# Eight softmax products of layer 0 go from VectorE to GpSimd, and the routing splits h earlier

## The chip, the cores and the metric

The kernel runs on one core of a Trainium2 chip. The metric is the device time of one execution in microseconds, as the median of several runs. Engines are named as the profile names them: PE (TensorE; PEld is its weight load), DVE (VectorE), ACT (ScalarE), POOL (GpSimd) and SP (SyncE, which issues most of the DMAs). L442 is line 442 of the kernel before.

## The reference

Two decoder layers over one sequence of 256 tokens with a model width of 1024. Layer 0's attention joins three branches: attention over compressed blocks, over selected blocks and over a window, each with a gate. Layer 1's attention is one masked softmax over all blocks. Behind each attention stands a mixture of 32 experts in 4 groups, of which a token takes one group and two experts, and then a gate with a per-layer embedding. Cut to what the change touches:

```python
# layer 0: two of the branches, a softmax each, scaled by a gate
p = exp(s - max(s)); p = p / sum(p)
o = gate_c * o_c + gate_s * (p_s @ v) + gate_w * (p_w @ v)
# routing, both layers
x = rms_norm(h, g_ffn)
scores = x @ w_router + bias           # 32 experts and 4 groups
group  = argmax(group scores); two best experts of that group
out   += sum over the two: weight * expert(x)
```

## The kernel before

**The whole.** Tokens lie in two query tiles of 128 rows (t = 0, 1). The program is written once, in order, with a tile framework: a scheduler decides when the program is built in which order each engine runs its instructions, and a pool of buffers decides which tile lies where. `tc.issue_after(x)` tells the scheduler to place what follows behind x. On the chip each engine runs its own list in that fixed order, and waits for semaphores where a tile isn't ready.

**Layer 0's attention** (`attend`, with nbr=2 branches) goes over eight chunks c of two heads (b = 0, 1). `scores` (L409 to L412, PE) multiplies queries by keys for chunk c+1; `turn` transposes the probabilities of chunk c on PE (L455 for p0, the first query tile; L456 and L457 for the two halves of p1, the second query tile) and copies them, L460 on ACT and L461 on DVE; `values` (L473 and L487, PE) multiplies them by the values. Between them stands `softmax`: for each head DVE adds the mask and takes the extreme (L429), ACT takes the exponential and its sum (L431), DVE makes the coefficients (L434 reciprocal, L436 times the gates), and each probability tile is multiplied by its coefficient. A head has four such products: p0 is 128x128 and p1 128x256, with two branches br each. In layer 0 the products of p0 run on POOL (L442) and those of p1 on DVE (L440). In layer 1 (nbr=1) all run on DVE.

In the same stage other work fills the engines: L301, L309, L311 and L315 normalise later queries, L340 splits weights into two parts (tiles wsp), L351 to L353 are products with split operands, L537 with L540 is the output projection, L571 a piece of the embedding's projection, L763 and L722 belong to the compressed branch.

**Routing** (both layers; L826 and on). h lies as rows of tokens. `transposed(t)` takes the mean square of h (ACT, L259 to L263: Square, Ln, Exp), transposes h on PE (L891) and copies the halves, L895 on DVE and L893 on ACT. `logits` multiplies by the router (L905) and DVE scales (L907). `choose(t)` finds group and experts on DVE (L913 to L923, the tile A marks the two experts). `order(t)` counts on PE (L936, L938) and makes each token's rank in its expert (L939), and `place` writes a 0/1 matrix from it (L929, tile rs). `gather_first` (L970, PE) gathers the tokens of the first eight experts with it; its other operand is h in two parts: h_hi, a cast of h (`split_h`, L948, ACT), and h_lo, what the cast leaves (`rest_h`, L951, DVE). Later L1021 gathers the others. L1045 (ACT) and L1047 (DVE) scale what was gathered, L1059 to L1088 make the experts' weights, L1094 and L1095 count tokens per expert, and `second_helping` finds experts with more than 32 tokens; the number of them, noveri (L1160), decides by a branch (L1308) if a leftover pass is run. Then `gate_up` (L1185) and `down` (L1215 to L1234) run over eight groups j of four experts, whose weights SP's queue loads (L840 gate and up, 1 MB each; L100 down, 0.5 MB).

The lines that set the two places are these:

```python
if t or nbr == 1:                    # softmax: which engine multiplies
    nc.vector.tensor_scalar(...)
else:
    mark["pool", c] = nc.gpsimd.tensor_scalar(...)
...
with tc.issue_after(nc.vector.tensor_tensor(A[:, t], A2[:, t, 0], A2[:, t, 1], ALU.add).ins):
    rest_h(t)                        # end of choose(t)
```

Of the kernel before, what the change touches and what calls it, by code (L numbers as in the profile page):

```python
# [15 lines left out]
ALU = mybir.AluOpType  # L16
# [23 lines left out]
def hybrid_kernel(ctx: ExitStack, tc: tile.TileContext, I: dict, out: bass.AP, dbg=None):  # L40
    nc = tc.nc
# [15 lines left out]
    def pa(shape, dt=F32):  # L57
        return ps.tile(shape, dt, tag="pa", name=nm("pa"))

    def pb(shape, dt=F32):  # L60
        return ps.tile(shape, dt, tag="pb", name=nm("pb"))

    def bt(tag, shape, dt=F32):

        return big.tile(shape, dt, tag=tag, name=nm(tag))

    def wt(tag, shape, dt=F32, bufs=None):
        return wk.tile(shape, dt, tag=tag, name=nm(tag), bufs=bufs)

    def st(tag, shape, dt=F32, bufs=None):  # L70
        return sm.tile(shape, dt, tag=tag, name=nm(tag), bufs=bufs)
# [183 lines left out]
    def columns(t):  # L255

        return hh[0][:, t, :].rearrange("q (k p) -> q k p", k=NK)

    def inv_rms(t, ss, rstd):  # L259
        junk = wt("sq", [P, D], BF16)  # L260
        nc.scalar.activation(junk, hh[0][:, t, :], AF.Square, accum_out=ss[:, t:t + 1])
        nc.scalar.activation(rstd[:, t:t + 1], ss[:, t:t + 1], AF.Ln, scale=1.0 / D, bias=eps_c)
        last_act.append(nc.scalar.activation(rstd[:, t:t + 1], rstd[:, t:t + 1], AF.Exp, scale=-0.5))  # L263
# [152 lines left out]
    def softmax(c, nbr, raw, gates=None):  # L416

        a, i = divmod(c, 4)
        ws = []
        for b in range(2):  # L420
            hh = 8 * a + 4 * b + i
            s0, s1 = raw[b]
            p1 = wt("p1", [P, nbr, S], bufs=4)
            p0 = wt("p0", [P, nbr, P], bufs=4)
            mx = st("mx", [P, NT, nbr], bufs=4)
            sums = st("sums", [P, NT, nbr], bufs=4)
            for t, (pt_, st_, dt_) in enumerate(((p0, s0, d_q0), (p1, s1, d_q1))):
                for br in range(nbr):
                    nc.vector.tensor_tensor_reduce(pt_[:, br, :], st_[:, br, :], dt_, -SLOPE[hh], 3e38,  # L429
                                                   ALU.add, ALU.min, accum_out=mx[:, t, br:br + 1])  # L430
                    mark["exp", c] = nc.scalar.activation(pt_[:, br, :], pt_[:, br, :], AF.Exp, bias=mx[:, t, br:br + 1],  # L431
                                         scale=-1.0, accum_out=sums[:, t, br:br + 1])
            cf = st("cf", [P, NT, nbr], bufs=4)
            nc.vector.reciprocal(cf, sums)  # L434
            if gates is not None:
                nc.vector.tensor_tensor(cf, cf, gates[:, :, 3 * hh + 1:3 * hh + 3], ALU.mult)  # L436
            for t, pt_ in enumerate((p0, p1)):
                for br in range(nbr):
                    if t or nbr == 1:
                        nc.vector.tensor_scalar(pt_[:, br, :], pt_[:, br, :], cf[:, t, br:br + 1], None, ALU.mult)  # L440
                    else:
                        mark["pool", c] = nc.gpsimd.tensor_scalar(pt_[:, br, :], pt_[:, br, :], cf[:, t, br:br + 1],  # L442
                                                                  None, ALU.mult)
            ws.append((p0, p1))
        return ws
# [54 lines left out]
    def attend(fill, after, nbr, qs, k1, k2, V, oT, gates=None, cmp=None):  # L500

        mark.clear()
        ws = softmax(0, nbr, scores(0, nbr, qs, k1, k2), gates)
        for c in range(8):
            fill(c)
            if nbr == 1:
                pts = turn(nbr, ws)
            if c < 7:
                raw = scores(c + 1, nbr, qs, k1, k2)
            if nbr == 2:  # L510
                pts = turn(nbr, ws)
            if c < 7:
                ws = softmax(c + 1, nbr, raw, gates)
            values(c, nbr, pts, V, oT, cmp)
            after(c)
# [86 lines left out]
    for j in range(2):  # L602
        pt = X.scaled(pts[j], "p1", 4)
# [74 lines left out]
    for c in range(2):  # L678
        pt = pb([P, P])
# [146 lines left out]
    def moe(l, out_proj_tail, prefetch):  # L826
# [38 lines left out]
        hT = bt("X3", [P, NK, S])  # L865
# [11 lines left out]
        A2 = st("A2", [P, NT, 2, NE], BF16, bufs=1)  # L877
        A = st("A", [P, NT, NE], BF16, bufs=1)
# [5 lines left out]

        def transposed(t):
            ts_ = slice(t * P, (t + 1) * P)
            inv_rms(t, ss, rstd)
            for k0 in range(0, NK, 4):
                pt = pa([P, 4, P])
                for k in range(4):  # L890
                    i = nc.tensor.transpose(pt[:, k, :], columns(t)[:, k0 + k, :], ident)  # L891
                if k0:
                    c = nc.scalar.copy(hT[:, k0:k0 + 4, ts_], pt)  # L893
                else:
                    nc.vector.tensor_copy(hT[:, k0:k0 + 4, ts_], pt)  # L895
            return i, c

        pls = {}
# [1 line left out]
        def logits(t, half):  # L900
            ts_ = slice(t * P, (t + 1) * P)
            if half == 0:
                pls[t] = pa([P, NE + NG])
            for k in range(4 * half, 4 * half + 4):
                i = nc.tensor.matmul(pls[t], hT[:, k, ts_], wr[:, l, k, :], start=(k == 0), stop=(k == NK - 1))  # L905
            if half == 1:
                nc.vector.scalar_tensor_tensor(lg[:, t, 0:NE + NG], pls[t], rstd[:, t:t + 1], rb[:, l, :], ALU.mult,  # L907
                                               ALU.add)
            return i

        def choose(t):

            nc.vector.max(gm[:, t], lg[:, t, NE:NE + 8])  # L913
            nc.vector.max_index(gi[:, t], gm[:, t], lg[:, t, NE:NE + 8])
            nc.vector.tensor_tensor(pen[:, t], iota_e[:, 0:NG], gi[:, t, 0:1].to_broadcast([P, NG]), ALU.not_equal)
            nc.vector.scalar_tensor_tensor(le[:, t].rearrange("p (g e) -> p g e", g=NG),
                                           pen[:, t, :, None].to_broadcast([P, NG, 8]), -BIG,
                                           lg[:, t, 0:NE].rearrange("p (g e) -> p g e", g=NG), ALU.mult, ALU.add)
            nc.vector.max(em[:, t], le[:, t])
            nc.vector.max_index(ei[:, t], em[:, t], le[:, t])  # L920
            nc.vector.tensor_tensor(A2[:, t], iota_e[:, None, :].to_broadcast([P, 2, NE]),
                                    ei[:, t, 0:2, None].to_broadcast([P, 2, NE]), ALU.is_equal)
            with tc.issue_after(nc.vector.tensor_tensor(A[:, t], A2[:, t, 0], A2[:, t, 1], ALU.add).ins):  # L923
                rest_h(t)

        def place(i, t):
            if t == 0:
# [19 lines left out]
        def split_h(t):  # L947
            nc.scalar.copy(h_hi[:, t], columns(t))  # L948

        def rest_h(t):  # L950
            nc.vector.tensor_tensor(h_lo[:, t], columns(t), h_hi[:, t].bitcast(F32), ALU.subtract)  # L951
# [22 lines left out]
        for n in range(2):  # L974
            out_proj_tail(0, n)
        out_proj_tail(1, 0)
        _, c = transposed(0)
        add, i = out_proj_tail(1, 1)
        with tc.issue_after(i.ins):
            i = logits(0, 0)  # L980
        with tc.issue_after(c.ins):
            split_h(0)
        with tc.issue_after(i.ins):
            i, c = transposed(1)
        with tc.issue_after(i.ins):
            i = logits(0, 1)
        with tc.issue_after(add.ins):
            choose(0)
        with tc.issue_after(c.ins):
            split_h(1)  # L990
        with tc.issue_after(i.ins):
            for k in range(2):
                i = logits(1, k)
# [8 lines left out]
        with tc.issue_after(i.ins):  # L1002
            for k0 in (0, 2):
                i = gather_first(0, k0)
        dump(f"h{1 + 3 * l}", hh[0])
        choose(1)
        with tc.issue_after(i.ins):
            i = order(1)
# [342 lines left out]
    def ple(B, X, nxt=None):  # L1351
# [36 lines left out]
        if nxt:  # L1388
            act_tables(EXP_LN, last_act[-1])

    B_p, X = moe(0, tail_a, lambda: load_ple(0))
    gm1 = g_mix[:, 1, :]
    B_kv = Weights(I["w_kv"], g_kv)
# [58 lines left out]

    attend(fill_b, after_b, 1, qs, k1, k2, V, oT)
    B_p, X = moe(1, partial(wo[0].add, 3), lambda: load_ple(1))
    dump("h5", hh[0])
    ple(B_p, X)
# [71 lines left out]
```

## Time and profile before

| what | value |
|---|---|
| median of 3 runs | 527.64 us (526.7 to 532.3) |
| profiled execution | 526.64 us, of which the span of the instructions is 524.9 |
| PE busy | 501.8 us (96%) |
| DVE busy | 339.8 us (65%) |
| ACT busy | 278.3 us (53%) |
| POOL busy | 50.9 us (10%) |
| granted clock of PE | 0.999 over the span |

The profile is of one execution. Busy is the time in which an engine had an instruction in work; waits are idle time of an engine just before an instruction, put down to what came last. Starts in the timeline are in us from the span's start. An entry such as "x2" in the timeline joins two neighbouring instructions of one form, and its time goes from the first's start to the last's end.

### The profile page before, as it was taken

How to read it: one execution, taken by the hardware profiler on the slowest of the kernel's cores; microseconds unless marked ns; L12 is line 12 of the kernel's file. 1: busy time of each engine (PE TensorE's matmuls, PEld its weight loads, DVE VectorE, ACT ScalarE, POOL GpSimd, SP SyncE). 2: the span in 40 equal slices, each digit the busy share in tenths (PEclk: the TensorE clock that was granted, in tenths of full speed). 3: DMA queues.
4: the chain of work that ended last, by engine and by line, in shares of the span. 5: the costliest groups of instructions: out<-in, count | busy, mean ns of one | idle time of the engine just before them, and what ended most of it. 6: DMA issues, size and time to landing. Idle time of an engine off the chain costs nothing. (4 is left out here: it accounts for less than half of the span.)

```text
span 524.9 us, 10142 instructions
## 1 busy us (share of the span) xinstructions
PE 501.8 (96%) x3784; PEld 355.7 (68%) x3784; DVE 339.8 (65%) x1038; ACT 278.3 (53%) x650; POOL 50.9 (10%) x120
## 2 busy tenths in 40 slices
PE   9989999999899999999899999999999999998996
PEld 6969899567568665555458999856567656554486
DVE  6759968989974853424269975787749525241593
ACT  6839747985654342312369975664444412231691
POOL 5000402234330001100000000000000003000000
PEclk9999999999999999999999999999999999999999
DMA  8976650006778899999993789632459899999902
GB/s 338 420 294 261 219 227 2 1 1 235 292 293 313 319 421 417 408 418 418 389 405 126 228 312 361 244 158 81 182 198 339 343 418 421 417 415 409 386 4 80
DMA packets 32213, 147.16 MB, mean 280 GB/s; under 512 B 4001, under 2 KB 4273, under 8 KB 22305
## 3 DMA queue, kind: packets, MB, share of 16 engines
q1 hardware_dynamic: 31232, 144.39, 70.6%
q0 software_dynamic: 784, 2.05, 1.0%
q8 instruction: 31, 0.51, 0.4%
q14 instruction: 22, 0.17, 0.1%
q10 hardware_dynamic: 144, 0.04, 0.0%
HBM read 146.98 MB, written 1.05 MB: 282 GB/s over the span
## 5 line engine op out<-in xcount | busy, mean ns | idle before, releaser
L131 DVE SCALAR_TENSOR_TENSOR wsp<-raw,vec,wsp 128x512 fp32r<-128x512 f32 (+1 forms) x96 | 67.1, 747 | 3.3 <-ACT wsp L130 3.2
L130 ACT ACTIVATE wsp<-raw,vec 128x512 fp32r<-128x512 f32 (+1 forms) x96 | 62.9, 719 | 2.3 <-DMA raw<-in_w_c_dram 1.6
L1185 PE MATMUL pb<-wgu,X 128*32 128x256 f32 x768 | 52.0, 381 | 0.6 <-PEq L1308 0.6
L431 ACT ACTIVATE p<-p,mx 128x128 f32<-128x128 f32 (+1 forms) x96 | 42.6, 445 | 10.2 <-DVE mx L429 10.1
L819 ACT ACTIVATE p<-pb,srs 128x128 f32<-128x128 f32 x16 | 5.9, 368 | 71.1 <-PE pb L1185 64.1
L1185 PEld LDWEIGHTS pb<-wgu,X 128*32 128x32 f32 x768 | 27.3, 110 | 18.5 <-issue 2.9
L340 DVE TENSOR_TENSOR pta<-pb,p 128x512 fp32r<-128x512 f32 (+1 forms) x36 | 24.7, 688 | 22.6 <-ACT p L340 18.1
L353 PE MATMUL pa<-XA,wsp 128*128 128x256 f32 x128 | 36.3, 284 | 2.1 <-DVE wsp L131 2.1
L351 PE MATMUL pa<-XA,wsp 128*128 128x256 f32 x128 | 37.2, 291 | 0.7 <-DVE rs L301 0.7
L822 DVE TENSOR_TENSOR p<-pb,ptb 128x128 f32<-128x128 f32 (+1 forms) x18 | 5.2, 289 | 48.4 <-ACT ptb L821 46.2
L352 PE MATMUL pa<-XB,wsp 128*128 128x256 f32 x128 | 36.2, 283 | 0.0
L340 ACT CAST p<-pb 128x512 fp32r<-128x512 f32 (+1 forms) x36 | 21.0, 586 | 27.8 <-PE pb L1234 27.8
L442 POOL TENSOR_SCALAR p<-p,cf 128x128 f32<-128x128 f32 x32 | 25.7, 815 | 65.6 <-DVE cf L436 46.8
L460 ACT COPY pta<-pa 128x512 f32<-128x512 f32 (+1 forms) x32 | 14.8, 479 | 30.4 <-PE pa L456 30.3
L429 DVE CUSTOM_DVE_ANT_0 p<-pb,d_q 128x128 f32<-128x128 f32 (+1 forms) x96 | 29.3, 351 | 2.2 <-PE pb L410 1.0
L1234 PE MATMUL pb<-wd,hT 128*32 128x512 f32 x224 | 29.3, 597 | 1.2 <-issue 0.4
L537 PE MATMUL pa<-wo,XH 128*128 128x512 f32 x64 | 29.4, 602 | 0.0
L1021 PE MATMUL pb<-rs,X 128*128 128x256 f32 (+1 forms) x192 | 26.6, 292 | 0.0
L1021 PEld LDWEIGHTS pb<-rs,X 128*128 128x128 f32 x192 | 24.3, 188 | 2.6 <-issue 2.5
L353 PEld LDWEIGHTS pa<-XA,wsp 128*128 128x128 f32 x128 | 24.1, 189 | 2.5 <-DVE wsp L131 2.5
L351 PEld LDWEIGHTS pa<-XA,wsp 128*128 128x128 f32 x128 | 24.1, 189 | 1.9 <-DVE rs L301 0.9
L352 PEld LDWEIGHTS pa<-XB,wsp 128*128 128x128 f32 x128 | 24.1, 189 | 0.5 <-issue 0.5
(373 smaller groups left out, 1348.6 us busy)
## 6 DMA issues: line engine op xcount, KB each, us to landing
wgu<-in_moe_gu_dram SPq DMA_DIRECT2D x48, 1024.0 KB, 11.8
wd<-in_moe_w_down_dram SPq DMA_DIRECT2D x48, 512.0 KB, 9.6
wo<-in_w_out_dram SPq DMA_DIRECT2D x8, 1024.0 KB, 4.7
raw<-in_ple_gate_dram SPq DMA_DIRECT2D x16, 512.0 KB, 7.0
raw<-in_a_q_dram SPq DMA_DIRECT2D x8, 512.0 KB, 7.3
XB<-in_moe_gu_dram SPq DMA_DIRECT2D x4, 1024.0 KB, 5.7
XA<-in_moe_gu_dram SPq DMA_DIRECT2D x4, 1024.0 KB, 6.8
X<-in_moe_gu_dram SPq DMA_DIRECT2D x4, 1024.0 KB, 5.3
```

The lines of the kernel that those rows point to most:

```text
L130: nc.scalar.activation(hi, src, AF.Copy, scale=g)
L131: nc.vector.scalar_tensor_tensor(lo, src, g, hi.bitcast(F32), ALU.mult, ALU.subtract)
L340: return nc.scalar.copy(hi, src), eng.tensor_tensor(lo, src, hi.bitcast(F32), ALU.subtract)
L351: nc.tensor.matmul(o, a[0], b[0], start=first, stop=False)
L352: nc.tensor.matmul(o, a[0], b[1], start=False, stop=False)
L353: return nc.tensor.matmul(o, a[1], b[0], start=False, stop=last)
L429: nc.vector.tensor_tensor_reduce(pt_[:, br, :], st_[:, br, :], dt_, -SLOPE[hh], 3e38, ALU.add, ALU.min, accum_out=mx[:, t, br:br + 1])
L431: mark["exp", c] = nc.scalar.activation(pt_[:, br, :], pt_[:, br, :], AF.Exp, bias=mx[:, t, br:br + 1], scale=-1.0, accum_out=sums[:, t, b ...
L537: m = nc.tensor.matmul(pt, self.oT[0][:, 2 * j + i, t * P:(t + 1) * P], self.raw[j][:, i, n * 512:(n + 1) * 512], start=(i == 0), stop=(i ...
L1021: nc.tensor.matmul(pt, part_columns(x, t)[:, k, :], Gs[i][:, t, 0:e1], start=(t == x == 0), stop=(t == x == 1))
L1185: last_ = nc.tensor.matmul(gu[32 * i:32 * i + 32, 0:2], xg[:, k, 32 * i:32 * i + 32], wgu[i][k], start=(k == 0), stop=(k == NK - 1), tile_ ...
L1234: behind[:] = [nc.tensor.matmul(ysp[32 * i:32 * i + 32, :], hT[:, 32 * i:32 * i + 32], wd[i][n], start=True, stop=True, tile_position=(0, ...
```

## The change

The condition in `softmax` leaves layer 1 as it is; in layer 0 DVE keeps, of the products of p1, only those with b=0 or br=0. The product for b=1, br=1 goes to POOL: one 128x256 product in each of the eight chunks. In the routing of both layers, `split_h(t)` is called first in `transposed(t)` instead of behind the copies, and `rest_h(t)` is placed behind DVE's copy in `transposed(t)` instead of behind the end of `choose(t)`.

```diff
                 for br in range(nbr):
-                    if t or nbr == 1:
+                    if (t and not b * br) or nbr == 1:
                         nc.vector.tensor_scalar(pt_[:, br, :], pt_[:, br, :], cf[:, t, br:br + 1], None, ALU.mult)
                     else:
...
         def transposed(t):
             ts_ = slice(t * P, (t + 1) * P)
+            split_h(t)
             inv_rms(t, ss, rstd)
...
-                    nc.vector.tensor_copy(hT[:, k0:k0 + 4, ts_], pt)
+                    d = nc.vector.tensor_copy(hT[:, k0:k0 + 4, ts_], pt)
+            with tc.issue_after(d.ins):
+                rest_h(t)
             return i, c
...
-            with tc.issue_after(nc.vector.tensor_tensor(A[:, t], A2[:, t, 0], A2[:, t, 1], ALU.add).ins):
-                rest_h(t)
+            nc.vector.tensor_tensor(A[:, t], A2[:, t, 0], A2[:, t, 1], ALU.add)
...
-        with tc.issue_after(c.ins):
-            split_h(0)
...
-        with tc.issue_after(c.ins):
-            split_h(1)
```

The scheduler's order changes with it, at three places that the prediction speaks of. The first is PE's order in layer 0's attention, at chunk c=1: p_164 and p_163 are p0 and p1 of head b=0, p_169 and p_168 those of b=1, and L311 with L409 and L410 begins the work for chunk c=2.

```order
+L487 MATMUL pa_1235<-X_46_396 128x256
 L455 MATMUL pa_1280<-ident,p_164_1198 128x128
-L763 MATMUL pb_1244<-ident,sq_1145 128x128 x2
+L456 MATMUL pa_1280<-ident,p_163_1197 128x128
+L455 MATMUL pa_1280<-ident,p_164_1198 128x128
+L456 MATMUL pa_1280<-ident,p_163_1197 128x128
+L457 MATMUL pa_1281<-ident,p_163_1197 128x128 x2
+L455 MATMUL pa_1292<-ident,p_169_1217 128x128
+L456 MATMUL pa_1292<-ident,p_168_1216 128x128
+L455 MATMUL pa_1292<-ident,p_169_1217 128x128
+L456 MATMUL pa_1292<-ident,p_168_1216 128x128
 L311 MATMUL pb_1255<-sq_1253,blk_114 128x512
```

The transposes of both heads, up to the last L456 of p_168, moved ahead of L311; before, all but the first stood behind the scores L409 to L412 of c=2.

The second place is DVE's order in layer 1's routing around the rank of the second token tile. Before (A is the choice of the second tile, X_994 is h_lo, es and ep belong to the experts' weights, rs is the matrix of `place`):

```order
-L921 TENSOR_TENSOR A_990_4702<-iota_e,ei_4700 128x64
-L923 TENSOR_TENSOR A_4703<-A_990_4702 128x32
-L951 TENSOR_TENSOR X_994_4706<-XA_2999,X_993_4705 128x1024
-L939 SCALAR_TENSOR_TENSOR rank_4704<-pa_4819,A_4703 128x32
-L1068 TENSOR_REDUCE es_4899<-ep_4893 128x2
-L929 TENSOR_TENSOR rs_4795<-rank_4704,iota_s 128x256
```

After, in the changed kernel's line numbers (L941 is the rank, L931 `place`):

```order
+L1069 TENSOR_REDUCE es_4899<-ep_4893 128x2
+L1070 TENSOR_TENSOR es_4899<-es_4899,gs_4897 128x2
+L1071 RECIPROCAL es_4899<-es_4899 128x2
+L1073 TENSOR_TENSOR cb_4906<-ep_4893,es_4899 128x4
+L1076 TENSOR_TENSOR oh_4701<-A_990_4702,cb_4906 128x2x32 x2
+L1078 TENSOR_TENSOR cw_4908<-oh_4701 128x64
+L1085 CAST R_4915<-cw_4908 128x16x4
+L1086 TENSOR_TENSOR R_4915<-cw_4908,R_4915 128x16x4
+L941 SCALAR_TENSOR_TENSOR rank_4704<-pa_4819,A_4703 128x32
+L931 TENSOR_TENSOR rs_4796<-rank_4704,iota_s 128x256
```

The remainder h_lo is gone from between choice and rank, and the chain of the experts' weights stands there instead. On PE, the counting matmul L1094 moved from between the gathers to behind the last of them.

The third place is SP's order in layer 1, ahead of the loads of the fourth group of experts (wgu, X, XB, XH and XA are buffers that take gate and up weights).

```order
 L100 DMA wd_5215<-in_moe_w_down_dram 128x1024
+L1305 TENSOR_LOAD noveri_4932
+L1305 ISA x2
+L840 DMA wgu_5288<-in_moe_gu_dram 128x2048
+L840 DMA XB_5201<-in_moe_gu_dram 128x2048
 L840 DMA X_1109_5203<-in_moe_gu_dram 128x2048
-L840 DMA XB_5201<-in_moe_gu_dram 128x2048
 L840 DMA XH_5205<-in_moe_gu_dram 128x2048
 L840 DMA XA_5207<-in_moe_gu_dram 128x2048
-L840 DMA wgu_5288<-in_moe_gu_dram 128x2048
```

The load of noveri into SP's register moved up from behind the last expert loads, and the branch on it moved up by the last gate-and-up loads and the down loads behind them.

## Rows read from the trace of the kernel before

**Rows 1.** The page, part 1: busy time, share of the span, instructions.

```profile
PE 501.8 (96%) x3784; PEld 355.7 (68%) x3784; DVE 339.8 (65%) x1038; ACT 278.3 (53%) x650; POOL 50.9 (10%) x120
```

**Rows 2.** Waits of PE by releaser: us in total, times, longest.

```profile
PE pa L473 <- ACT pta L460: 1.9, 4, 0.6
```

**Rows 3.** Windows: length; busy us (instructions) by engine, clock, DMA share, GB/s.

```profile
95.00:107.00 12.00, 12.00 (x64) 8.03 (x65) 10.44 (x41) 11.39 (x33) 3.54 (x5) 1.00 0.00 1
...
131.00:143.00 12.00, 10.41 (x71) 7.09 (x70) 10.88 (x48) 7.74 (x28) 3.74 (x4) 1.00 0.71 276
143.00:161.00 18.00, 17.45 (x100) 12.46 (x101) 11.36 (x48) 9.09 (x33) 5.38 (x9) 1.00 0.78 292
```

**Rows 4.** Line L455: what PE idled for before it (us, times).

```profile
  POOL p L442: 1.5, 4
```

**Rows 5.** Timeline, c=2: start, us, engine, line, [idle before, releaser].

```profile
106.79 1.27 POOL L442 TENSOR_SCALAR p<-p,cf 128x128 f32<-128x128 f32 x2 [1.03 <-DVE cf L436]
...
109.60 0.27 PE L456 MATMUL pa<-ident,p 128*128 128x128 f32 x1
```

**Rows 6.** Timeline, c=5, c=6 and c=7: last pair of products, last L456.

```profile
138.11 2.06 POOL L442 TENSOR_SCALAR p<-p,cf 128x128 f32<-128x128 f32 x2
...
139.11 0.67 DVE L340 TENSOR_TENSOR wsp<-wo,wsp 128x512 fp32r<-128x512 f32 x1
...
140.39 0.27 PE L456 MATMUL pa<-ident,p 128*128 128x128 f32 x1
...
146.79 1.27 POOL L442 TENSOR_SCALAR p<-p,cf 128x128 f32<-128x128 f32 x2 [1.38 <-DVE cf L436]
...
148.29 0.27 PE L456 MATMUL pa<-ident,p 128*128 128x128 f32 x1
...
154.25 1.30 POOL L442 TENSOR_SCALAR p<-p,cf 128x128 f32<-128x128 f32 x2 [2.65 <-DVE cf L436]
...
155.87 0.27 PE L456 MATMUL pa<-ident,p 128*128 128x128 f32 x1
```

**Rows 7.** POOL: L442's durations min/median/max in ns; a 128x256 select (busy us, mean ns).

```profile
L442 POOL TENSOR_SCALAR p<-p,cf x32: 597/720/1471, 83.3 to 154.9; 128x128 f32<-128x128 f32 x32
...
L183 POOL TENSOR_SCALAR_AFFINE_SELECT d_q<-d_q 128x256 f32<-128x256 f32 x1 | 0.9, 865 | 0.0
```

**Rows 8.** DVE's products in 83 to 161, by form: busy us, mean ns.

```profile
L440 DVE TENSOR_SCALAR p<-p,cf 128x256 f32<-128x256 f32 x32 | 11.3, 393 | 0.1
```

**Rows 9.** Timeline, c=1.

```profile
94.88 0.69 PE L487 MATMUL pa<-X 32*128 32x256 f32 x2
...
95.00 0.66 DVE L301 TENSOR_TENSOR rs<-pa,rrow 128x512 f32<-128x512 f32 x1
...
95.98 1.64 POOL L442 TENSOR_SCALAR p<-p,cf 128x128 f32<-128x128 f32 x2 [1.75 <-ACT wsp L340]
...
97.01 0.27 PE L456 MATMUL pa<-ident,p 128*128 128x128 f32 x1
```

**Rows 10.** Layer 1's routing: ACT's casts (min/median/max in ns), and the timeline.

```profile
L948 ACT CAST X<-XA x2: 1031/1039/1047, 390.3 to 394.0; 128x1024 fp32r<-128x1024 f32 x2
...
400.11 1.22 DVE L951 TENSOR_TENSOR X<-XA,X 128x1024 fp32r<-128x1024 f32 x1
...
401.25 0.18 DVE L939 SCALAR_TENSOR_TENSOR rank<-pa,A 128x32 f32<-128x32 f32 x1
...
398.94 1.51 PE L970 MATMUL pb<-rs,X 128*128 128x256 f32 x8
...
402.04 2.13 PE L970 MATMUL pb<-rs,X 128*128 128x256 f32 x16 [0.39 <-DVE es L1069]
```

**Rows 11.** Layer 1's expert stage: timeline, and a window (columns as rows 3).

```profile
407.06 0.15 DVE L1160 CAST noveri<-nover 128x1 int32<-128x1 f32 x1
...
407.80 0.33 SPq L840 DMA_DIRECT2D X<-in_moe_gu_dram  x1
...
460.00:486.00 26.00, 23.78 (x221) 12.73 (x220) 8.42 (x27) 6.97 (x16) 0.00 (x0) 1.00 1.02 412
```

## The prediction

> **What bounds the kernel now.** I read the page's totals first: PE is busy for 501.8 of 524.9 us [rows 1], so a change can win at most what PE idles, and it loses whatever makes PE wait anew. Next come the waits of PE by what released them; of the attention the largest entry is 1.9 us in four pieces, for ACT's copy of transposed products [rows 2]. So no single wait is long there. Then the windows over layer 0's attention, about a chunk each, where the softmax edit works [rows 3]. PE is busy for 12.00 of 12 us in 95 to 107 and loses 1.59 us in 131 to 143. DVE stands at 10.44 and 10.88 of 12 us there and falls to 11.36 of 18 behind; POOL has 3.5 to 5.4 us of work in each. By these totals moving work from DVE to POOL looks free. The question is when POOL's products are due.
>
> **When POOL's products are due.** In each chunk the transposes of head b=1 read what POOL writes last. The waits behind one of these lines show PE waiting for POOL four times, 1.5 us in all [rows 4]. The timeline says in which chunks. In c=2 the second pair of products ends at 106.79 + 1.27 = 108.06, and the last L456 (transpose of p1, b=1, br=1, the tile that the new product writes) starts at 109.60: 1.54 us of room [rows 5]; c=0, 3 and 4 read the same way have more. In c=5 the pair ends at 138.11 + 2.06 = 140.17 against 140.39, in c=6 at 148.06 against 148.29, in c=7 at 154.25 + 1.30 = 155.55 against 155.87 [rows 6]. So in the last three chunks POOL is already last, with 0.22, 0.23 and 0.32 us to the reader.
>
> **The price D of one new product.** No row shows POOL multiplying 128x256. From below: a 128x128 product took 0.597 us at least [rows 7], and since the work is only added to POOL it can't be a gain there. From above: a product of a slow pair took 2.06 / 2 = 1.03 us [rows 6], and twice the elements at that pace are 2.06 us. Between them lies POOL's own 128x256 row, a select, at 0.865 us [rows 7]. I take D = 0.95 us, near that row with a little for slow neighbours, and keep 0.6 and 2.06 for the range.
>
> A pair takes 1.27 us in c=6 and 2.06 us in c=5, where DVE runs an L340 (0.67 us) in the middle of it [rows 6]. The Trainium skill, page "SBUF — State Buffer", section "SBUF: two separate sides", says that VectorE and GpSimd share one pair of ports: a GpSimd instruction, or a VectorE one with two SBUF inputs, takes it for its whole length, and the other one blocks. The trace agrees in kind: the pair beside the L340 is 0.79 us longer. By that rule the new product costs D plus one L340 wherever one runs, and holds DVE up in return, which speaks against the change; rival E below is this case.
>
> **Part 1, softmax.** It takes eight 128x256 products from DVE, 0.393 us each [rows 8], 3.1 us together, and gives POOL eight.
> - c=0 and c=2 to 4: the room, 1.54 us or more [rows 5], exceeds D, so PE sees nothing of it. If D is 2.06, c=2 gives 0.5 us.
> - c=5 to 7: behind the last L456 follow L457, ACT's copy L460 and the value products, nothing else being ready, so each chunk ends later by D less its room: 3 x 0.95 - (0.22 + 0.23 + 0.32) = +2.1 us.
> - c=1: here PE's order changes too. Before, L311, L487 and the eight score products of c=2 ran while POOL multiplied (95.98 to 97.62), and the transposes came just behind, from 97.01 [rows 9]. Now the transposes of both heads, the L456 of p_168 (POOL's new product) included, stand ahead of L311 and the scores. DVE's coefficients come sooner, because its L301, which ran 95.00 to 95.66 between the reciprocal and the product with the gates [rows 9], is moved: I put POOL's pair at 95.3, its end at 96.6 to 96.9 (1.3 to 1.64 us long) and the new product's at about 97.7. PE is there early. Without the two L311 in front (about 1 us), L487 ends at 94.88 + 0.69 - 1.0 = 94.6; nine transposes at a start every 0.11 us bring it to 95.6. So PE idles for about 2.1 us, where it idled for none [rows 3], and the scores of c=2, with DVE's softmax behind them, come that much later. I take +2.0 us; from below 0.8 (both products at their fastest, and part of it caught up in PE's idle time behind), from above 3.1 (D = 2.06).
> - DVE's relief: 0.39 us a chunk counts only where DVE ends last and POOL doesn't, c=2 to 4. Three of them are 1.2 us; I count -1.0. Its ends are nothing and all eight, -3.1.
>
> **Parts 2 and 3, routing, in both layers.** What goes: an L951 of 1.22 us stood between the choice of the second token tile and its rank. It started at 400.11, the rank ran only at 401.25, and then PE waited for 0.39 us, up to 402.04, to gather with it [rows 10]. What comes: the casts of 1.04 us [rows 10] stand ahead of the squares on ACT, which still ends before DVE asks; the other L951 lands between the first tile's logits and its choice, so that this choice starts 1.1 us later; and the dozen short rows that make the experts' weights now stand ahead of the second rank. I walked DVE's new order with the old durations: the first tile's rank comes 1.6 us later than before, and with it the first gathers, 398.94 before [rows 10], at about 400.2. PE has its L571 to fill until about 399.5, so a hole of 0.7 us is left. The second rank comes about 0.5 us later than 401.25, and the gathers behind it at 402.45 instead of 402.04. The counting matmul L1094 goes from inside the gathers to just ahead of gate_up, where nothing runs beside it (0.2 us). That makes +0.3 to +0.7; I take +0.5 per layer, +1.0 in all. If the old wait of 0.39 us went and nothing came, it would be -0.8; the worst end is +1.8.
>
> **SP's queue, layer 1.** The load of noveri moves ahead of the loads of the j=3 experts. DVE writes noveri at 407.06, and those loads were issued from 407.80 [rows 11], so with the routing's delay they start a little later. Layer 1's DMA is full from there to the end (1.02 of its share in 460 to 486, rows 11), so a late stream passes through: +0.2 us, from 0 to 1.0. The branch, moved ahead of the last loads on SP, I cost at nothing, since the transfers queued ahead of it keep the DMA busy; if they don't, it is rival D.
>
> **Sum.** 2.0 + 2.1 - 1.0 + 1.0 + 0.2 = +4.3 us on the profiled execution's 526.64 us (its span of 524.9 and 1.74 around it): 530.9. The median of the runs, 527.64, lies 1.0 us above that execution; I add a third of it: **531.2 us**.
>
> **The rivals.**
> - B, hidden: POOL works at its fast pace alone (D = 0.6), and a late chunk is caught up in PE's idle time behind it. For it: POOL idles two thirds of each window [rows 3]. Against: the last three chunks have 0.3 us of room [rows 6]. Terms: c=1 0.8, c=5 to 7 3 x 0.6 - 0.77 = 1.0, relief -1.0, routing 0 and SP 0: 526.64 + 0.8 + 0.3 = 527.7.
> - C, the other side: DVE paces the chunks c=1 to 4 and the softmax of each next one, so that each removed product shortens a chunk by its 0.39 us: -3.1, and in the routing the two waits of 0.39 go: 526.64 - 3.1 - 0.8 = 522.7; with c=5 to 7 giving 1.0 back, 523.7. It decides from the point where POOL's product is there before PE asks for it; against it stand rows 6.
> - D, SP holds layer 1's stream: the chain behind noveri on DVE, or the branch, comes later than I think, and the full DMA passes on 3 us more: 534.2.
> - E, the lock: every new product takes 2.06 us. Then c=5 to 7 give 3 x 2.06 - 0.77 = 5.4, c=1 gives 3.1, c=2 0.5, with no relief and routing and SP as above: 5.4 + 3.1 + 0.5 + 1.2 = +10.2, 536.8. For it: the slow pair of c=5. Against: in c=2, 6 and 7 the pairs take 1.27 to 1.30 [rows 5, 6].
>
> **How the numbers follow.** A (the sum) 0.50, B 0.20, C 0.13, D 0.07, E 0.10. One per cent, 5.3 us, is about what a measurement of this kernel can tell from no change, which puts the bounds at 522.4 and 532.9. Faster needs C at its best: 0.06. Slower takes D, E and the upper fifth of A (whose own range is 528.5 to 534): 0.07 + 0.10 + 0.10 = 0.27. Same is the rest, 0.67. The range, 524.3 to 535.8, leaves out the better half of C and most of E.
>
> **What would show it.** In the changed kernel's profile: L442 with 40 instructions, eight of them 128x256 near 0.95 us; new waits of PE for POOL at L456, about 2 us in c=1 (its window no longer full) and 0.7 us in each of c=5 to 7; in c=2 to 4 a little less idle time of PE. In the routing no L951 between choice and rank, a hole of 0.7 us ahead of the first gathers, and gate_up 0.3 to 0.7 us later after them. On SP the j=3 loads are less than 1 us late. I am wrong if POOL's 128x256 takes 0.6 or 2 us, if PE's wait in c=1 is under 1 us, or if the routing gets shorter.

## The result, and the profile after

The changed kernel takes 0.82% longer: the ratio to the kernel before is 1.0082, with a 95% interval from 1.0060 to 1.0103 (20 runs of each; medians 533.93 and 528.96 us). The ratio leaves out two of these 20 runs of the changed kernel (536.88 and 538.40 us, at the lowest clocks), which count as slow, while the medians are over all. On 528.96 us the ratio is +4.3 us, the size that the prediction's sum had. The profiled execution shown here, 533.5 us, has a span of 531.8 us, 6.9 more than before's; not all of these 6.9 us belong to the change, as the stages below show.

The page's totals and POOL's products by form (busy us, mean ns, then idle time before and its releasers), after:

```profile
PE 504.0 (95%) x3784; PEld 357.3 (67%) x3784; DVE 339.2 (64%) x1030; ACT 278.9 (52%) x650; POOL 57.8 (11%) x128
...
L442 POOL TENSOR_SCALAR p<-p,cf 128x128 f32<-128x128 f32 x32 | 24.1, 763 | 62.8 <-DVE cf L436 48.9 <-PE pa L353 9.1 <-ACT p L431 3.9
L442 POOL TENSOR_SCALAR p<-p,cf 128x256 f32<-128x256 f32 x8 | 8.6, 1074 | 0.0
```

POOL has its eight products more, at 1.07 us in the mean. DVE is busy for 0.6 us less, not 3.1. Its rows together are 3.1 us shorter (397.5 to 394.4 us), and in the attention it is busy for 2.4 us less; ahead of it and behind it, fewer of its rows overlap. What it does beside POOL does not take longer: the sixteen L340 of the attention add up to 10.9 us before and 11.0 after. PE's waits by releaser, those that were not there before (compare [rows 2]):

```profile
PE pa L456 <- POOL p L442: 2.6, 3, 1.6
...
PE pb L1183 <- issue: 1.9, 1, 1.9
```

L456 waits for POOL's new product three times, 2.6 us, the longest 1.6 us, and that one is in c=1. Before, no matmul waited for POOL by this view: the 1.5 us of [rows 4] are idle time of the weight load (PEld), which the view of a line counts as well. The windows answer to [rows 3]; the later two are shifted by what the stage has lost by then, so only the first is compared:

```profile
95.00:107.00 12.00, 10.30 (x48) 5.90 (x47) 8.10 (x28) 8.58 (x21) 3.22 (x3) 0.86 0.00 0
131.00:143.00 12.00, 11.59 (x69) 8.76 (x67) 10.64 (x40) 5.12 (x20) 6.12 (x8) 1.00 0.62 205
143.00:161.00 18.00, 15.98 (x98) 11.40 (x96) 13.75 (x59) 10.92 (x39) 8.82 (x14) 1.00 0.82 316
```

In 95 to 107 PE lost 1.70 us where it lost none. The last column but two is new too: the granted clock is 0.86 of full there. Its timeline, with POOL's three products and PE's wait for the third (to set beside [rows 9]):

```profile
96.35 3.22 POOL L442 TENSOR_SCALAR p<-p,cf 128x128 f32<-128x128 f32 x3 [1.35 <-DVE cf L436]
...
97.74 0.33 PE L455 MATMUL pa<-ident,p 128*128 128x128 f32 x1
99.62 0.48 PE L456 MATMUL pa<-ident,p 128*128 128x128 f32 x1 [1.55 <-POOL p L442]
99.89 1.92 PE L311 MATMUL pb<-sq,blk 128*128 128x512 f32 x2
100.82 1.42 PE L409 MATMUL pb<-X,X 128*128 128x512 f32 x1
```

and short windows over the same stretch:

```profile
97.00:99.00 2.00, 0.93 (x5) 0.34 (x3) 1.86 (x4) 0.81 (x2) 2.00 (x3) 1.00 0.00 0
99.00:100.00 1.00, 0.38 (x2) 0.38 (x3) 0.00 (x0) 0.00 (x0) 0.57 (x1) 0.65 0.00 0
100.00:101.00 1.00, 1.00 (x4) 0.48 (x3) 0.00 (x0) 0.81 (x2) 0.00 (x0) 0.50 0.00 0
101.00:102.00 1.00, 1.00 (x2) 0.42 (x2) 0.00 (x0) 0.46 (x2) 0.00 (x0) 0.50 0.00 0
102.00:103.00 1.00, 1.00 (x5) 0.87 (x4) 0.30 (x1) 1.00 (x3) 0.00 (x0) 0.64 0.00 0
```

POOL worked from 96.35 to 99.57. PE stood still from 98.07 to 99.62, and in that idle time its clock went from 2.4 to 1.2 GHz (0.50 of full) and stayed there for some three microseconds. The two L311, which had taken 1.02 us, took 1.92. So the wait was paid twice.

Stage by stage, the profiled execution after is longer than before by 0.9 us ahead of the attention (where both programs have the same work, and where the profiles of the other kernels below differ by -0.7 to +0.7), by 4.0 us in layer 0's attention, by 0.45 us in the two routings, and by 2.5 us in layer 0's expert stage, of which 1.9 us is one stop of PE that the waits call "issue", in the last gate_up. Layer 1's expert stage is 1.1 us shorter, which the part on the prediction comes back to. The rest, 0.1 us, lies in the stretches between. Six of the ten experiments of the first table and both of the last two show that stop too in their profiles (1.1 to 2.5 us), among them kernels that don't take longer than before; before's profile does not. It is put aside here, since it comes with and without a loss; one profile of each kernel can't show if it belongs to the kernel or to the execution.

### The profile page after: what moved, and what is told of

Read it like the earlier page. It is cut to its first block, busy times and chain, and to the rows that moved or that the text cites. A ratio compares the mean times of both kernels' runs of the same rounds, so it can differ in the third digit from the quotient of the medians.

```text
span 531.8 us, 10141 instructions
## 1 busy us (share of the span) xinstructions
PE 504.0 (95%) x3784; PEld 357.3 (67%) x3784; DVE 339.2 (64%) x1030; ACT 278.9 (52%) x650; POOL 57.8 (11%) x128
## 3 DMA queue, kind: packets, MB, share of 16 engines
q0 software_dynamic: 784, 2.05, 1.0%
HBM read 146.98 MB, written 1.05 MB: 278 GB/s over the span
## 4 chain that ended last, share of the span: by engine, by line
PE 38%; DMA 7%; DVE 3%; ACT 1%; issue 1%; SPq 0%; DVEq 0%; ACTq 0%
PE pa L537 5%; DMA wgu<-in_moe_gu_dram 5%; PE pb L1183 4%; PE pa L353 4%; PE pa L351 4%; PE pa L352 3%; PE pb L1232 3%; PE pa L1220 3%; DMA wd<-in_moe_w_down_dram 2%; PE pb L1019 1%; PE pb L353 1%; PE pb L352 1%; PE pb L351 1%; PE pa L473 1%; PE pb L311 1%
## 5 line engine op out<-in xcount | busy, mean ns | idle before, releaser
L442 POOL TENSOR_SCALAR p<-p,cf 128x128 f32<-128x128 f32 (+1 forms) x40 | 32.5, 825 | 62.8 <-DVE cf L436 48.9
L340 DVE TENSOR_TENSOR pta<-pb,p 128x512 fp32r<-128x512 f32 (+1 forms) x36 | 24.7, 688 | 21.3 <-ACT p L340 17.7
L340 ACT CAST p<-pb 128x512 fp32r<-128x512 f32 (+1 forms) x36 | 20.9, 585 | 26.4 <-PE pb L1232 26.2
L1232 PE MATMUL pb<-wd,hT 128*32 128x512 f32 x224 | 28.8, 597 | 0.9 <-DMA wd<-in_moe_w_down_dram 0.5
```

The costliest lines, as they stand in the source:

```text
L340: return nc.scalar.copy(hi, src), eng.tensor_tensor(lo, src, hi.bitcast(F32), ALU.subtract)
L1232: behind[:] = [nc.tensor.matmul(ysp[32 * i:32 * i + 32, :], hT[:, 32 * i:32 * i + 32], wd[i][n], start=True, stop=True, tile_position=(0, ...
```

## The experiments

The attention stage is measured from the first L409 to the first transpose of layer 0's routing (L891; a higher number where lines are added ahead of it): 78.03 to 163.33 before, 85.30 us, and 78.94 to 168.26 after, 89.32 us. Each run also comes with its mean granted clock over the span; a low clock is counted here where it is 0.996 or less (some 4 us at half speed). In every profile the clock is also at half in the last 0 to 2.8 us of the span, which enters the mean, and a run without a trace doesn't tell where its clock fell. Of the runs of the kernel before, 2 of 29 have one beside the first four experiments, 3 of 27 beside the next four and 0 of 23 beside the others.

| kernel | ratio, 95% | attention, us against before | runs with a low clock |
|---|---|---|---|
| after | 1.0082 (1.0060 to 1.0103) | +4.0, clock fell in c=1 | 16 of 20 |
| softmax part alone | 1.0111 (1.0068 to 1.0153) | +2.6, clock 1 | 4 of 6 |
| routing part alone | 1.0009 (0.9977 to 1.0040) | 0.0 | 3 of 12 |
| product of c=0 alone | 0.9982 (0.9962 to 1.0002) | 0.0 | 0 of 12 |
| products of c=1 to 7 | 1.0035 (1.0007 to 1.0064) | +3.8, clock fell behind c=5 | 7 of 12 |
| products of c=5 to 7 | 1.0104 (1.0059 to 1.0149) | +2.6, clock fell behind c=5 | 5 of 5 |
| product of head b=0 | 1.0044 (1.0014 to 1.0075) | +0.1, clock 1 | 5 of 11 |
| c=1 to 7, PE filled | 1.0054 (1.0026 to 1.0081) | +1.6, clock 1 | 2 of 11 |
| whole change, c=1 in old order | 1.0049 (1.0012 to 1.0086) | +1.5, clock 1 (it fell behind the stop in layer 0's last gate_up) | 5 of 11 |
| one product less on POOL | 0.9985 (0.9961 to 1.0008) | -1.0, clock 1 | 1 of 12 |
| c=2 to 4 more, c=5 to 7 less | 0.9995 (0.9976 to 1.0013) | -1.25, clock 1 | 0 of 12 |

**Each part alone.** The theory after the result: the softmax part carries the loss, by PE's waits for POOL and the lower clock behind them; the rival: the routing carries it.

```diff
# softmax part alone: this edit on the kernel before
-                    if t or nbr == 1:
+                    if (t and not b * br) or nbr == 1:
# routing part alone: the changed kernel with this edit undone
```

> The softmax part alone, routing as before. If the softmax carries the loss (theory: PE's waits for POOL and the lower clock behind them), the ratio is within 0.2% of the changed kernel's, about 1.007, with the window 95 to 107 short of 12 us of PE work by over 1 us and a granted clock under 1 in it. If the routing carries it, the ratio is within 0.2% of 1.

> The routing part alone. By the sum of the prediction +1.0 us (1.002); by the changed kernel's trace, where each layer's stage is 0.2 us longer, +0.5 us (1.001). If the routing carried the loss, 1.005 or more. The granted clock stays as before.

Softmax alone 1.0111, routing alone 1.0009. The softmax carries the loss: the two intervals lie apart. Its ratio is 0.3% above the changed kernel's, where 0.2% was expected, but it has six runs only and the intervals overlap; the routing's part is too small for the times, though its trace shows the two routings longer (+0.2 and +0.5 us). In softmax alone the window 95 to 107 lacks 1.70 us of PE's work, as expected, but the profiled execution kept its clock at 1 there: the expected fall did not show in it, while four of the six runs had a low clock. The same waits with and without a fall give the fall's price: 4.0 - 2.6 = 1.4 us.

**Which chunk: c=0, or all the others.** In the changed kernel's order, the transposes ahead of the scores in c=1 come from the product of c=0: with it alone on POOL the scheduler writes the same order, and without it the old one.

```diff
-                    if t or nbr == 1:
+                    if (t and not (b * br and c == 0)) or nbr == 1:    # c=0 alone
+                    if (t and not (b * br and c)) or nbr == 1:         # c=1 to 7
```

> POOL takes the product in chunk c=0 alone. PE's order at c=1 is the changed kernel's, with the transposes ahead of the scores, but POOL has no product to add there. If that order is what costs, c=1 still waits for POOL's pair by 0.5 to 1 us and the run is +1 to +3 us (1.002 to 1.006); if the new product in c=1 is what costs, at most +1 us (1.002).

> POOL takes the product in c=1 to c=7, and PE's order at c=1 stays that of before. Theory order: most of the loss goes, what is left is c=5 to 7 with +1 to +2 us less the relief of DVE, 1.000 to 1.003, and the granted clock in 95 to 107 is 1. Theory POOL's product as such: the waits stay in c=1 and c=5 to 7, 1.005 or more.

The order by itself costs nothing (0.9982; PE is busy for 11.83 of 12 us in 95 to 107). By the traces it costs where it meets POOL's product in c=1. Without c=0, 1.0035 is left, a little over the upper end that the theory gave. The clock in c=1 was 1, but it fell elsewhere; the windows behind c=5 in this kernel's profile:

```profile
137.00:140.00 3.00, 2.79 (x18) 2.13 (x16) 3.00 (x10) 1.17 (x4) 3.00 (x4) 1.00 0.68 221
140.00:143.00 3.00, 1.69 (x12) 1.02 (x14) 2.03 (x10) 1.33 (x5) 1.12 (x2) 0.99 1.03 434
143.00:146.00 3.00, 3.00 (x15) 1.84 (x12) 2.81 (x19) 3.00 (x15) 1.02 (x2) 0.50 0.93 393
146.00:149.00 3.00, 3.00 (x9) 2.41 (x9) 0.14 (x1) 0.69 (x3) 0.24 (x1) 0.50 0.00 0
149.00:152.00 3.00, 3.00 (x17) 2.49 (x16) 1.82 (x10) 1.44 (x6) 1.25 (x3) 0.87 0.24 44
```

PE had 1.31 us of idle time in 140 to 143, part of it the wait for POOL's new product, and then worked at 1.2 GHz to about 150. Every matmul of that stretch is longer; from the last L456 of c=5 to the first of c=6 it is 8.8 us here, 5.6 before and 5.7 in softmax alone at a clock of 1, so the lower clock cost 3.1 us there. The five runs of this kernel with a clock of 0.998 or more have a median of 528.9 us, which is before's.

**The last three chunks alone, and another head.**

```diff
-                    if t or nbr == 1:
+                    if (t and not (b * br and c >= 5)) or nbr == 1:    # c=5 to 7
+                    if (t and (b or not br)) or nbr == 1:              # head b=0
```

> POOL takes the product in c=5 to 7 alone; PE's order is that of before but for one transpose. Theory waits: two or three new waits of PE for POOL, 0.4 to 0.7 us each, +1.1 us in all (1.002), granted clock 1 throughout. Theory clock: the waits stand behind the idle time that PE has in 131 to 143 already, so in some runs the granted clock falls to 0.5 behind c=5 for some us, and these runs are +3 to +5 us: ratio about 1.004 with a spread of 7 us.

> POOL takes the product of head b=0, br=1, in all eight chunks, so that it stands between POOL's two pairs instead of behind the second. In c=6 and 7 POOL idles 1.4 to 2.7 us between the pairs, which covers 0.87 to 1.1 us; where it idles less (c=0, c=5) the second pair comes up to 1 us later. Theory last-in-the-queue: less wait than the changed kernel's softmax, 0.999 to 1.002, clock 1. Theory amount of work on POOL: as the softmax alone, 1.006 or more.

Three products alone lose as much as the whole change: 1.0104, with a low clock in all five runs. The kernel with c=1 to 7 has these three too and came to 1.0035 with seven low clocks of twelve, so between these two the size of the loss goes with how many runs have a low clock, and five runs are few. The waits named in the trace are 1.1 us, two of up to 0.6; they come on top of the idle time that PE had before.

```profile
131.00:143.00 12.00, 9.99 (x61) 6.76 (x61) 10.01 (x42) 6.84 (x24) 4.44 (x5) 0.98 0.72 279
143.00:146.00 3.00, 3.00 (x16) 1.66 (x12) 2.85 (x18) 3.00 (x14) 0.95 (x2) 0.53 0.92 388
```

PE is at 9.99 of 12 us, where before had 10.41 [rows 3], and the clock falls behind. With head b=0's product the stage costs only 0.1 us while the clock stays, as expected of a product between the pairs; but PE's window 131 to 143 has 9.90 of 12 us here too. Its eleven runs fall into two groups: six with a clock of 0.998 or more, 526.8 to 529.6 us, and five with 0.994 to 0.996, 531.2 to 533.0 us. So the ratio of 1.0044, which lies between the two theories, is not the stage's own length; most of what it is above the expected 1.002 comes from the five runs with the lower clock (the other six have a median of 528.7 us, 0.25% above before's 527.4). Where the clock fell in those five is not shown: the trace is of a run at a clock of 1.

**PE kept busy, and the old order in c=1.**

```diff
# c=1 to 7, PE filled: FILL = {5: 8, 6: 4, 7: 8}
                 nc.tensor.transpose(ta[:, br, 0:P], p0[:, br, :], ident)
+                for _ in range(b * br * FILL.get(c, 0)):
+                    nc.tensor.transpose(ta[:, br, P:S], ident, ident)
...
# whole change, c=1 in old order: L456 of c=1, b=1, br=1 behind the last of the scores
+                if c == 1 and b * br:
+                    with tc.issue_after(mark["sc"].ins):
+                        nc.tensor.transpose(ta[:, br, P:S], p1[:, br, 0:P], ident)
```

> The product on POOL in c=1 to c=7, as in the run without c=0, and PE multiplies the identity 8, 4 and 8 times (0.11 us each, into space that is overwritten) while it waits for POOL's product in c=5, 6 and 7. Theory clock: PE has more to do and yet the runs get faster, because the granted clock stays at 1 behind c=5: median clock 0.998 or more and 1.000 to 1.002. Theory waits: nothing gained, 1.0035 or a little more, as without the filling.

> The whole change, with one constraint of order: in c=1 the last transposes of p1, b=1, br=1 stand behind the scores of c=2, as before. Theory order at c=1: PE's wait for POOL of 1.6 us in c=1 goes, the granted clock there stays 1, and what is left is c=0, c=5 to 7 and the routing: +1.5 to +2.5 us (1.003 to 1.005). Theory product as such: no change against the changed kernel, 1.008.

With 20 matmuls more on PE the profiled execution's attention is 2.2 us shorter than without them (+1.6 instead of +3.8), the clock in 143 to 161 is 1.00 instead of 0.81, and a low clock is down from seven of twelve runs to two of eleven. The times did not follow: 1.0054 against 1.0035 without the filling, with intervals that overlap, and runs at a clock of 0.999 took 531 us. So the filling keeps the clock, but that this buys time for whole runs is not shown. In the kernel with c=1 in the old order the wait of 1.6 us is gone (the longest for POOL is 0.6), the stage is at +1.5 us instead of the +2.6 of softmax alone, both at a clock of 1 in the stage, and the ratio is 1.0049, which is in the range that theory gave; the interval reaches 1.0086, so the times alone would not separate it from the changed kernel. In this profile the clock fell from 2.4 to 1.2 GHz at 263.7 us, behind the stop of 2.5 us in layer 0's last gate_up: a low clock in a run need not come from the attention.

**The other direction.** If POOL's last product decides, taking one away from it in c=5 to 7 should gain.

```diff
-                    if t or nbr == 1:
+                    if t or nbr == 1 or (b * br and c >= 5):           # one product less on POOL
+                    if (t and not (b * br and 2 <= c <= 4)) or nbr == 1 or (b * br and c >= 5):   # c=2 to 4 more
```

> The other direction on the kernel before: in c=5 to 7 POOL's product of p0 for b=1, br=1 goes to DVE, so that POOL ends 0.65 us sooner. Theory last-in-the-queue: PE's waits for POOL at L455 (1.5 us in four) shrink to under 0.5 us, the attention is 0.5 to 1.2 us shorter and the clock stays 1: 0.998 to 0.999. Theory DVE: DVE becomes the last and the time is the same or longer, 1.000 to 1.002.

> POOL takes one product more in c=2 to 4, where it has 1.5 us or more of room, and one less in c=5 to 7, where it has none; routing as before. If room decides: as the reverse run or 0.2 us better, 0.997 to 0.999. If any product added to POOL costs, 1.002 or more.

What the weight loads (PEld) of the kernel with one product less still wait for POOL at L455, in the attention (83 to 165 us; [rows 4] has 1.5 us in four):

```profile
PEld pa L455 <- POOL p L442: 0.8, 2, 0.6
```

The waits ahead of the last transposes of c=5 and c=7 are gone; 0.61 us in c=1 and 0.16 us at the first pair of c=5 are left, so the total is above the 0.5 us expected. The stage is 1.0 us shorter; with the three extra products of c=2 to 4, 1.25 us. This is what the theory says of room. The times, 0.9985 and 0.9995, are not clear of 1, and the second, outside its 0.997 to 0.999, doesn't show the 0.2 us that it was to add.

**The routing's two halves**, one run each, whose times say nothing. The expectations count from the first L571; the numbers below count first from the first logits (L905), since the first L571 itself turned out to start later behind them.

```diff
# cast first
+            split_h(t)                       # first in transposed(t), no longer behind the copies
# remainders early: rest_h(t) behind split_h(t), no longer behind choose(t)
```

> The cast first, remainders at their old place. If the remainder's move is what lengthens the stage, the stage of each layer from the first L571 to the first gate_up is as before (8.41 us) within 0.1 us; if the cast on ACT is, it is 0.2 us longer, as in the changed kernel.

> The remainders behind ACT's copy and cast, casts at their old place. If the remainder's move off the path between choice and rank were a gain by itself, PE's wait of 0.39 us ahead of the second tile's gathers goes and the stage is 0.2 to 0.4 us shorter than 8.41 us; if the weights' chain takes its place, the wait stays and the stage is the same or up to 0.4 us longer.

From the first L905 to the first gate_up, before takes 12.72 us in both layers, after 12.95 and 12.94, cast first 12.90 and 13.10, remainders early 12.47 and 12.90. So the cast makes the stage longer by 0.2 to 0.4 us, and the remainder alone gains 0.25 us in layer 0 and loses 0.2 in layer 1: its gain is not firm. From the first L571, the mark of the expectations, before takes 8.4 us in both layers. The cast's stage is 8.45 us in layer 0, within 0.1 us, which the expectation took as a sign that the cast is free (the delay is ahead of that mark), and 8.65 in layer 1. The remainder's is 7.99 and 7.82, and PE's wait ahead of the second gathers is gone in both layers, as the theory of a gain by itself said: in that kernel the chain of the weights stays behind the rank. What it loses in layer 1 is ahead of the mark, where L571 starts 0.8 us later.

## Why the prediction was right

Forecast 531.2 us against 527.64, or +4.3 us by the sum against the profiled execution; measured +0.82%, on before's 528.96 us +4.3 us, with the sign forecast and inside the range. The place was right: PE waits for POOL's product in c=1 and in the last chunks. That the size agrees is luck in good part: at a clock of 1 the terms measure about +1.9 us (attention +2.6, routing +0.45, layer 1's expert stage -1.1), and the four runs of the changed kernel with a clock of 0.997 or more have a median of 530.6 us, 1.7 above before's. The sixteen others, at a lower clock, have 534.8.

- **c=5 to 7 (+2.1) was too large as a wait, and right as a place.** POOL is last there, as read from the 0.2 to 0.3 us of room ([rows 4], read as PE's wait, is the weight load's): PE waits for POOL at L456 in c=5 and c=6, for 1.1 us in all. In softmax alone, at a clock of 1, the lag behind before goes from 1.72 us at the last L456 of c=4 to 2.16 in c=5 and 2.90 in c=6, and back to 2.57 in c=7, so it grows by 0.85 us. The product itself took 0.92 us there, close to the 0.95 chosen. But in c=5 the pair ahead of it is 0.2 us shorter, since DVE multiplies once less beside it, and in c=7 POOL starts its second pair 1.65 us later than before where PE is 2.9 us late, so that chunk catches up.
- **c=1 (+2.0) was right in size** for the wait: 1.55 us, and at the last value products of c=2 softmax alone lags by 1.85 us, c=0 alone by 0.1. The cause is the one given, order and product together: at the last L456 of c=2 softmax alone lags by 2.05 us, c=0 alone by 0.3, c=1 to 7, with the old order, by 0.5, and the whole change with its last transpose in the old place by 1.05. With c=0 and c=1 both on POOL, c=3 has a wait of 0.6 us for POOL at L455 too, where the sum had room; with c=0 alone or c=1 to 7 it has none. The new product took more than the 0.95 us that I chose: here it is 1.9 us, with two L340 of DVE beside it. The price was chosen with some luck: the select that it leaned on, 0.865 us before, took 0.497 us in the profile after, and 2.06 us was no upper bound, since [rows 7] has a 128x128 product of 1.47.
- **c=0 (nothing) was wrong by 0.9 us at its own end, but it is paid back.** DVE ran three L340 in a row beside POOL's products, and POOL's three took 3.63 us instead of 2.19 for two; but PE did not wait for them. With c=0 alone POOL ended at 89.29, and PE's transposes of head b=1 waited for DVE's copy L461, in an order that changed in c=0 too:

```profile
90.26 0.30 PE L455 MATMUL pa<-ident,p 128*128 128x128 f32 x1 [0.61 <-DVE ptb L461]
```

  With c=0 alone the stage as a whole ends where before's does.
- **DVE's relief (-1.0)**: 0.25 us is what the three extra products of c=2 to 4 gave to the kernel with one less in c=5 to 7. Together the four terms of the attention were +3.1; at a clock of 1 it measured +2.6.
- **The routing (+1.0) was twice too large**: +0.23 and +0.22. The walk along DVE's new order added whole durations; the trace has rows that don't depend on one another starting 0.07 to 0.1 us apart. The first tile's rank came 0.7 us later instead of 1.6, and the first gathers 0.3 instead of 1.2. The hole of 0.7 us ahead of the first gathers did not come. PE's wait ahead of the second gathers stayed (0.38 us in layer 0 and 0.45 in layer 1, instead of 0.39 [rows 10]): the weights' chain took the place of the remainder, as forecast.
- **SP (+0.2) had the wrong sign.** The j=3 loads went out 0.34 us later, counted from layer 1's first logits, and nothing behind them was late. From the first gate_up of layer 1 to the start of its last down product (L1234; L1232 after) it is 88.5 us before and 87.3 after, all of the difference behind the last gate_up. Before, PE stopped there twice, once until SP's branch on noveri:

```profile
485.31 1.06 PE L1234 MATMUL pb<-wd,hT 128*32 128x512 f32 x8 [0.39 <-SPq L1308]
486.78 1.07 PE L1234 MATMUL pb<-wd,hT 128*32 128x512 f32 x8 [0.40 <-issue]
```

  After, both stops are gone, and one of 0.48 us for the down weights is there. All five kernels with an edit of the routing, in which SP loads noveri earlier, take 87.2 to 87.4 us, and the nine others 88.1 to 90.0. The branch's new place, which the sum cost at nothing, is the likely cause; no run moves it alone.

What the sum had no term for is the clock. PE's clock, which the prediction took as full in every stretch, was lower in 16 of the 20 runs. In three profiles (the changed kernel, c=1 to 7, c=5 to 7) it fell in or behind the new idle time; it added 1.4 us in the first (c=1) and 3.1 us in the second (c=5). That it fell at the same places in the runs without a trace is not shown. Rival E, the lock, has its row (1.9 us beside L340) but not its size: the mean product took 1.07 us. DVE was not held up in return: its two L340 beside the 1.9 us took 0.68 us each, back to back. Of rival B the price of 0.6 us did not show, but its other half did: the late chunks c=0 and c=7 were caught up behind. Of C nothing showed in the attention; D's stream was not held.

## What to carry to other kernels

Ask of an idle engine when its results are due, not how busy it is: POOL had 10% of work, and in three of eight chunks its last product was ready only 0.2 to 0.3 us before PE read behind it. A product moved there pays where the reader has room behind it (c=2 to 4) and costs where it has none (c=5 to 7), and one edit can change a scheduler's order in a chunk that it doesn't touch, or on a queue far behind, for better or worse. Look at PE's granted clock in every window where a change adds idle time: the second bill may be as large as the wait.

## What was not expected of the hardware

PE's clock reacted to little. It fell from 2.4 to 1.2 GHz inside one idle stretch of 1.55 us (c=1), and behind a window in which PE was still busy for 9.99 of 12 us with no wait of over 0.6 us (c=5 to 7 alone). With the same idle stretch in softmax alone, and with 9.90 of 12 us in the same window with head b=0's product, the profile shows it at 2.4 GHz throughout the attention. The same kernel kept its clock in some runs and not in others, 3 to 4 us apart. What decides between them in a given run stays open, and so does the stop of 1.1 to 2.5 us named "issue" in the last gate_up of layer 0, which comes and goes between profiles of kernels with the same order there.
